# One attention layer with eight gates: where ScalarE's SiLU may begin, where two mixed heads are staged, and which transfer leaves first

## The chip, the cores and the metric

The kernel runs on one core of a Trainium2 chip. The metric is the device time of one execution in microseconds (us); lower is better. TensorE (PE) multiplies matrices, PEld is its weight load, VectorE (DVE) and ScalarE (ACT) do elementwise work, GpSimd (POOL) does a little of it and issues accumulating transfers, and SyncE (SP) issues most DMAs.

## What is computed

One layer (DEPTH is 1) of a trunk on 512 positions of width 2048, in float32. The reference, cut to its core:

```
h    = rms_norm(x, norm_g)
proj = h @ w_in                      # 2048 -> 8192: qA kA vA gA | qB kB vB gB
ya   = stick_breaking_attention(split_heads(qa, 8), split_heads(ka, 8), split_heads(va, 8))
yb   = chunk_band_attention(split_heads(qb, 8), split_heads(kb, 8), split_heads(vb, 8),
                            q_norm_g, k_norm_g, rel_bias)
mixed = concat([merge_heads(ya) * silu(ga), merge_heads(yb) * silu(gb)])
x     = x + mixed @ w_out            # 2048 -> 2048
```

Stick-breaking attention has no softmax: it takes log-sigmoids, a reversed running sum along the keys and one exponential. The chunked attention normalizes queries and keys per head, adds a bias by clipped distance and takes a softmax.

## The kernel before

The input projection is cut into 32 units of 256 columns, `u = 4 * g + kind`: eight groups g (two heads each), and in each group the kinds query, key, value and gate. The result of a unit is a tile `c` of 128 x 2 x 512. Products are Strassen-Winograd: seven half-size products in the place of eight, with sums of weight blocks (`s1` to `s4`) and of activation blocks (`T1` to `T4`) made on DVE. Every operand is split into a high part (a copy by ACT into the type `fp32r`) and a low part (the remainder, a subtraction by DVE), and a product is up to three matmuls. So a block of weights is ready for PE when ACT's cast (L571, for later steps L450) and behind it DVE's subtraction (L572, L454) are done.

**The running chain.** Units 3 to 30 of the sequence are "major": they go through seven stages p0 to p6, each a full product of 4 x 4 matmuls (L831 with 512 columns, L833 with 256). Stages accumulate in three banks of PSUM: p0, p2, p4 and p6 go on in one bank, p1 and p3 in a second, p5 in a third. Between them, `chain(m)` copies intermediate sums out, into a workspace `c` of four parts in the arena (`CMB`):

- `c0` (L593): after p0, and p2 may not start before it.
- `c3` (L596): after p1, and p3 may not start before it.
- `c2` (L599): after p2, and p4 may not start before it.
- The first and second of the three DVE joins (L601) after p3 and p4; p6 waits for the second one. Then the third after p5, the copy `c1` (L612) after p6, and the sum of the unit (L616).

The workspace `CMB` takes parts 20 to 28 of the arena (in units of 256 columns), and `UU`, which the units of the other kind use for their sums, parts 26 to 28: the last quarter of `CMB`. `chain` claims all of `CMB` at once before `c0`.

**Attention and gates** of a group run beside the units of the next group, in the gaps of the same engines: `prep_b` (norms of queries and keys, after a transpose), `v_turn` (transposed values, scaled by L1499), `score`, `turn`, `values`. `gates(g)` multiplies the gate tile by the norm of x on DVE (L1548) and then runs one ACT operation of three instructions (L1551, L1552): a load of the table that holds SiLU, the SiLU itself, and a load of the table with logarithm and exponential, which all other ACT work uses. `values` needs the gates for its last product; where they are not done yet, it first copies its bank to SBUF (L1532).

**The output projection** (units 32 to 35, `NU` being 32) multiplies the mixed heads, which went to DRAM (`mixd`) and come back as eight tiles j = 0 to 7. Each is loaded in two DMAs (L672, L673) into a staging place named by `HOME[j]`, and split there (L745, L746) into `x`. A place is free for its next user when the splits of its last one are done. The first output unit takes the heads in the order of j, eight products of three matmuls each.

**Order.** Nothing of the order is written out. A planner in the kernel (`schedule`) runs a clock with a cost for each operation; whenever an engine is free in that clock it takes the ready operation that is due first. `Op(engine, cost, fn, due)` is one such entry; without a due time it is due 4.5 us after it became ready (`LATE`), and `need(k, before)` is due so long before product k begins by the plan. What comes out is a fixed order on each engine, and each engine goes through its own in order.

**The start.** SP's first DMA loads the norm's gains `ng_t` (L130); then come, by due time, the first weights and the tiles of x. The two halves of x's first tile are issued on ACT's queue (L672, L673). Eight matmuls on zeros (L1562) run while they come in.

Of the kernel before, what the change touches and what calls it, by code (L numbers as in the profile page):

```python
# [11 lines left out]
AF = mybir.ActivationFunctionType  # L12
# [62 lines left out]
def trunk_kernel(ctx: ExitStack, tc: tile.TileContext, xT, xn, wi, wqk, wo, ng, qg, kg, rel, out):  # L75
# [50 lines left out]
    banks = ps.tile([P, 8, S], F32, tag="banks", name="banks")  # L126
    halves = banks.rearrange("p a (b c) -> p (a b) c", c=H)
    mixd = [dp.tile([P, S], F32, tag=f"mixd{i}", name=f"mixd{i}") for i in range(2 * NG)]

    sp.dma_start(ng_t, ng)  # L130

    KB = 256
    arena = single([P, 28 * KB], "arena")
# [8 lines left out]
    def avail(r):  # L142

        return all(r[1] <= x[0] or x[1] <= r[0] for x in taken.values())

    def claim(key, r):
        assert avail(r), (key, r, taken)
        taken[key] = r
        return arena[:, r[0]:r[1]] if r[0] < 100 * KB else parts[:, r[0] - 100 * KB:r[1] - 100 * KB]
# [39 lines left out]
    def AC(w, fn, due=None, n=1):  # L189
        return Op("ACT", (0.085 + 0.85e-3 * w) * n, fn, due)  # L190
# [389 lines left out]
    def chain(m):  # L580
        u = MAJOR[m]
        b = [banks[:, major_bank(u, p), :] for p in (0, 1, 5)]
        k = [at_step[stage(m, p)] for p in range(NP)]
        there = lambda p: lambda: ("stage", m, p) in done

        def free(p):
            x = major_bank(u, p)
            del holder[2 * x], holder[2 * x + 1]

        yield there(0)  # L590
        yield lambda: avail(CMB)
        c = claim(("cmb", m), CMB).rearrange("p (a b) -> p a b", a=4)
        yield AC(512, lambda: act.copy(c[:, 0, :], b[0]), need(k[2], AHEAD[5]))  # L593
        done.add(("before", m, 2))
        yield there(1)
        yield AC(512, lambda: act.copy(c[:, 3, :], b[1]), need(k[3], AHEAD[5]))  # L596
        done.add(("before", m, 3))
        yield there(2)
        yield AC(512, lambda: act.copy(c[:, 2, :], b[0]), need(k[4], AHEAD[5]))  # L599
        done.add(("before", m, 4))  # L600
        join = lambda i, x, y, op=ALU.subtract: lambda: dve.tensor_tensor(out=c[:, i, :], in0=x, in1=y, op=op)  # L601
        yield there(3)
        yield DV(512, join(2, b[1], c[:, 2, :]), clock[0] + 3)
        free(1)
        yield there(4)
        yield DV(512, join(3, c[:, 3, :], b[0]), need(k[6], AHEAD[6]))
        done.add(("before", m, 6))
        yield there(5)
        yield DV(512, join(0, b[2], c[:, 0, :], ALU.add), clock[0] + 3)
        free(5)  # L610
        yield there(6)
        yield AC(512, lambda: act.copy(c[:, 1, :], b[0]), clock[0] + 1)  # L612
        free(0)
        _, t = yield from result(u, 0)
        t_ = t.rearrange("p a (b c) -> p (a b) c", c=H)
        yield DV(1024, lambda: dve.tensor_tensor(out=t_, in0=c[:, :, :H], in1=c[:, :, H:], op=ALU.add), clock[0] + 1.5)  # L616
        unclaim(("cmb", m))
        done.add(("unit", u))

    X = {}  # L620
    XB, xb_tiles, staged = {}, {}, {}
    STAGE = "qk", "qk", "cq", "ck", "cv", "cg"

    HOME = "cq", "ck", "qk", "cq", "cv", "cg", "cq", "qk"
    SUMS = "qk", "qk", "qk", "qk", "qk", "ck", "qk", "ck"


# [12 lines left out]
    def activations(j, mixed):  # L640
# [23 lines left out]
        else:  # L664
# [5 lines left out]

        queue, engine = (act, "ACT") if j == 0 and not mixed else (sp, "SP")
        first = lambda: queue.dma_start(r.rearrange("p (a b) -> p a b", b=H)[:, 0:4:3, :], a.rearrange("p (a b) -> p a b", b=H))  # L672
        second = lambda: queue.dma_start(r[:, H:3 * H], b)  # L673
        one = ("B11",), f(h[:, :1]), f(l[:, :1])
        spawn(raw(j, mixed, Op(engine, 0.47, first, need(k, 10), lag=P * 2048), r, k,
                  [(0, 1) + one] + ([(3, 4, ("B12",)) + ((f(h[:, 6:]), f(l[:, 6:])) if not mixed else (None, None))] if not mixed or plain(NU, j) else []), j, not mixed, kt, dt), (0, 0, j))
        spawn(raw(j, mixed, Op(engine, 0.47, second, need(k + 2 * mixed, 9), lag=P * 2048), r, k + 2,
                  [(1, 3, ("B21", "B22"), f(h[:, 1:3]), f(l[:, 1:3]))], j + NJ, not mixed, kt, dt), (0, 0, j))
        yield lambda: all(("scaled", j, i, mixed) in done for i in (j, j + NJ))
        if mixed:  # L680
# [675 lines left out]
    def prep_b(g, kind, h):  # L1356

        n = head(g, h)
        yield lambda: "R" in done and ("unit", 4 * g + kind) in done
        yield lambda: all(("read", n - 1, k) in done for k in range(2)) if h else kind == 0 or ("read", n, 0) in done  # L1360
        yield lambda: not h or kind == 0 or ("read", n, 0) in done
        k, = yield from buffer("L")
        t_ = tmp([P, S], "L", "tm")
        i = yield from take(("forth", g, kind, h))
        f = C[g, kind][:, h, :]
        b = banks[:, i, :]

        def turn_(src):
            for t in range(NT):
                pe.transpose(b[:, t * P:(t + 1) * P], src[:, t * P:(t + 1) * P], ident)  # L1370

        yield M(0.5, lambda: turn_(f))

        def squares():
            for t in range(NT):
                act.activation(t_[:, t * P:(t + 1) * P], b[:, t * P:(t + 1) * P], AF.Square,
                               accum_out=ssq[:, kind, h, t:t + 1])

        yield Op("ACT", 2.0, squares)
        if kind == 0:  # L1380
            give(i)
        done.add(("read", n, kind))
        v, y = vq[:, kind, h, :], rq[:, kind, h, :]

        def norms():
            dve.tensor_tensor(out=v, in0=ssq[:, kind, h, :], in1=rstd2, op=ALU.mult)
            dve.tensor_scalar(out=v, in0=v, scalar1=1.0 / HD, scalar2=EPS, op0=ALU.mult, op1=ALU.add)

        yield DV(4, norms, n=3)
        yield from rsqrt(v, y, NT)  # L1390
        yield DV(4, lambda: dve.tensor_tensor(out=y, in0=y, in1=rstd, op=ALU.mult))
        if kind == 0:

            drop("L", k)

            def both():
                dve.tensor_scalar(out=yn[:, h, :], in0=y, scalar1=-1.0, scalar2=None, op0=ALU.mult)
                dve.reciprocal(out=yi[:, h, :], in_=y)

            yield DV(4, both, n=2)  # L1400
            done.add(("factor", n))
            return

        def scaled():
            for t in range(NT):
                act.activation(t_[:, t * P:(t + 1) * P], b[:, t * P:(t + 1) * P], AF.Copy, scale=y[:, t:t + 1])

        yield Op("ACT", 1.5, scaled)
        d = yield from qk_of(g, h)
        yield M(0.5, lambda: turn_(t_))  # L1410
        drop("L", k)
        yield from heads(n, 1, d, b, kg_t)
        give(i)
# [69 lines left out]
    def v_turn(g, h):  # L1483
        n = head(g, h)
        yield lambda: "R" in done and ("unit", 4 * g + 2) in done
        yield lambda: ("values", n - 1) in done if n else all(("staged", j, 0) in done for j in range(NJ))
        i = yield from take(("v", g, h))
        f = C[g, 2][:, h, :]
        b = banks[:, i, :]

        def fn():
            for t in range(NT):
                pe.transpose(b[:, t * P:(t + 1) * P], f[:, t * P:(t + 1) * P], ident)  # L1493

        yield M(0.5, fn)

        def scaled():
            for t in range(NT):
                act.activation(f[:, t * P:(t + 1) * P], b[:, t * P:(t + 1) * P], AF.Copy, scale=rstd[:, t:t + 1])  # L1499

        yield Op("ACT", 1.25, scaled)
        give(i)
        d = vv[n] = tmp([P, 2, S], "v", "v", F32R)
        yield AC(512, lambda: act.copy(d[:, 0, :], f))
        yield DV(512, lambda: dve.tensor_tensor(out=d[:, 1, :], in0=f, in1=d[:, 0, :].bitcast(F32), op=ALU.subtract))
        done.add(("v read", n))
        done.add(("v", g, h))

    def values(g, h):
# [32 lines left out]
        yield L_(P * 2048, lambda: sp.dma_start(mixd[(1 - g % 2) * NJ + g // 2 * 2 + h], f))  # L1542
        done.add(("store", g, h))

    def gates(g):
        yield lambda: "R" in done and ("unit", 4 * g + 3) in done
        f = C[g, 3]
        yield DV(1024, lambda: dve.tensor_tensor(out=f, in0=f, in1=R[:, None, :].to_broadcast([P, 2, S]), op=ALU.mult))  # L1548

        def silu():  # L1550
            act.activation(f, f, AF.Silu)  # L1551
            act.preload_act_table_set(TABLES)  # L1552

        yield Op("ACT", 3.7, silu)
        done.add(("gates", g))


# [10 lines left out]
                       pattern=[[-1, P]], channel_multiplier=1)  # L1568

    def constants():  # L1570
        yield Op("ACT", 1.28, lambda: act.preload_act_table_set(TABLES), -5.0)

        yield lambda: position[0] > 20

        def gains():
            sp.dma_start(qg_t, qg)
            sp.dma_start(kg_t, kg)

        yield Op("SP", 0.94, gains, 25.0)
        yield lambda: position[0] > 60  # L1580
        yield DV(1, lambda: dve.tensor_scalar(out=qgs, in0=qg_t, scalar1=SCALE, scalar2=None, op0=ALU.mult), 40.0)
# [71 lines left out]
```

## Time and profile before

| | us |
|---|---|
| median of 3 runs (913.51 to 915.98) | 914.37 |
| the profiled execution | 913.6 |
| its span, first to last instruction | 911.8 |
| PE busy | 899.8 (99%) |
| PEld busy | 802.1 (88%) |
| DVE busy | 768.9 (84%) |
| ACT busy | 636.7 (70%) |
| SiLU blocks on ACT: table load, SiLU, table load | 8, first at 102.3, last at 742.7 |

The span is the time between the first and the last instruction that the profiler saw; the execution takes 1.8 us more than that. A busy PE has matmuls in flight, which are pipelined: the start of one matmul to the start of the next says more than their lengths, and the idle time of PEld (the weight load ahead of each matmul) shows where PE waited for its operands.

### The profile page before, as it was taken

The numbers are of one execution on the slowest core, as the hardware profiler recorded it, in microseconds if no ns is written. First come the engines' busy times: TensorE is split into PE (matmuls) and PEld (weight loads), VectorE is DVE, ScalarE is ACT, GpSimd is POOL, SyncE is SP. The second block draws the span as 40 slices with busy tenths as digits, with TensorE's granted clock in tenths as the row PEclk, the third lists the DMA queues.
The fourth block names the chain that finished last, engine by engine and source line by source line (L and its number), as shares of the span: only waits on it lengthen the run. The fifth ranks groups of instructions, "written<-read, shape, count | busy, mean of one in ns | idle before, by whom it ended". The sixth has DMA issues, their size and how long they took to land.

```text
span 911.8 us, 15413 instructions
## 1 busy us (share of the span) xinstructions
PE 899.8 (99%) x5504; PEld 802.1 (88%) x5504; DVE 768.9 (84%) x1253; ACT 636.7 (70%) x1199; POOL 66.4 (7%) x91
## 2 busy tenths in 40 slices
PE   9999999999999999999999999999999999999997
PEld 6898888888888888888888888888888987899997
DVE  8989898788897887888978878889878988988785
ACT  8776967886687758775877587768868885534342
POOL 0001010000010100010001000010000000101011
PEclk9999999999999999999999999999999999999999
DMA  9677696566766886767667867676665536656371
GB/s 322 208 220 176 147 218 163 139 171 168 182 157 151 191 199 147 179 172 178 159 147 185 206 151 176 173 176 161 158 160 134 173 128 197 168 179 181 120 186 47
DMA packets 187549, 156.22 MB, mean 171 GB/s; under 512 B 9040, under 2 KB 157008, under 8 KB 187472
## 3 DMA queue, kind: packets, MB, share of 16 engines
q1 hardware_dynamic: 177264, 122.20, 44.0%
q0 software_dynamic: 9792, 32.51, 21.5%
q8 instruction: 43, 0.70, 0.3%
q10 hardware_dynamic: 416, 0.52, 0.2%
q14 instruction: 34, 0.28, 0.1%
HBM read 117.45 MB, written 8.39 MB: 138 GB/s over the span
## 4 chain that ended last, share of the span: by engine, by line
PE 85%; ACT 6%; DVE 5%; issue 2%; DMA 2%; DVEq 0%; SPq 0%; ACTq 0%
PE banks L831 35%; PE banks L760 18%; PE banks L833 17%; PE banks L758 9%; PE banks L821 2%; PE banks L1470 2%; DVE parts L572 1%; PE banks L1370 1%; ACT parts L571 1%; PE banks L822 1%; DMA arena<-in_wi 1%; ACT L1552 1%; DVE arena L540 1%; PE banks L1493 1%; ACT L1551 1%
## 5 line engine op out<-in xcount | busy, mean ns | idle before, releaser
L831 PE MATMUL banks<-x,parts 128*128 128x512 f32 x1568 | 502.5, 402 | 3.9 <-ACT arena L596 2.7
L833 PEld LDWEIGHTS banks<-x,parts 128*128 128x128 f32 x1568 | 294.5, 188 | 69.7
L833 PE MATMUL banks<-x,parts 128*128 128x256 f32 x1568 | 309.7, 279 | 0.0
L572 DVE TENSOR_TENSOR parts<-arena,parts 128x1024 fp32r<-128x1024 f32 x196 | 239.3, 1222 | 68.5 <-ACT parts L571 66.8
L571 ACT CAST parts<-arena 128x1024 fp32r<-128x1024 f32 x196 | 206.6, 1055 | 119.9 <-PE banks L831 85.1
L831 PEld LDWEIGHTS banks<-x,parts 128*128 128x128 f32 x1568 | 240.8, 189 | 6.4 <-ACT arena L596 4.0
L760 PE MATMUL banks<-parts,x 128*128 128x256 f32 (+1 forms) x672 | 135.1, 299 | 1.4 <-DVE x L746 1.4
L450 ACT CAST parts<-arena 128x1024 fp32r<-128x1024 f32 (+3 forms) x84 | 77.5, 928 | 75.9 <-PE banks L760 40.3
L760 PEld LDWEIGHTS banks<-parts,x 128*128 128x128 f32 x672 | 107.5, 191 | 5.9 <-DVE x L746 2.2
L454 DVE TENSOR_TENSOR parts<-arena,parts 128x1024 fp32r<-128x1024 f32 (+3 forms) x84 | 89.4, 1069 | 20.3 <-ACT parts L450 20.0
L758 PE MATMUL banks<-parts,x 128*128 128x256 f32 (+1 forms) x336 | 100.4, 299 | 0.0
L760 PE MATMUL banks<-x,parts 128*128 128x256 f32 (+1 forms) x320 | 75.6, 328 | 0.2 <-DVE parts L454 0.2
L540 DVE TENSOR_TENSOR arena<-arena 128x1024 f32<-128x1024 f32 x56 | 68.2, 1217 | 4.1 <-DMA arena<-in_wi 4.0
L758 PEld LDWEIGHTS banks<-parts,x 128*128 128x128 f32 x336 | 63.9, 190 | 3.2
L760 PEld LDWEIGHTS banks<-x,parts 128*128 128x128 f32 x320 | 53.9, 190 | 7.0 <-DVE parts L454 2.0
L532 POOL DMA_DIRECT2D arena<-arena x28 | 24.5, 875 | 415.9 <-DMA arena<-in_wi 119.9
L758 PE MATMUL banks<-x,parts 128*128 128x256 f32 (+1 forms) x160 | 52.8, 330 | 0.0
L601 DVE TENSOR_TENSOR arena<-banks,arena 128x512 f32<-128x512 f32 x56 | 38.3, 684 | 4.3 <-PE banks L833 4.1
L551 POOL DMA_DIRECT2D arena<-arena x28 | 24.4, 870 | 219.9 <-DVE parts L572 176.6
L616 DVE TENSOR_TENSOR c<-arena 128x1024 f32<-128x1024 f32 x28 | 34.1, 1217 | 0.3 <-ACT arena L612 0.2
L758 PEld LDWEIGHTS banks<-x,parts 128*128 128x128 f32 x160 | 30.5, 190 | 3.1 <-ACT parts L450 0.5
L1479 DVE TENSOR_TENSOR wtl<-banks,wth 128x128 fp32r<-128x128 f32 (+1 forms) x64 | 30.9, 483 | 1.6 <-ACT wth L1478 1.5
(210 smaller groups left out, 1156.1 us busy)
## 6 DMA issues: line engine op xcount, KB each, us to landing
arena<-in_wi SPq DMA_DIRECT2D x310, 256.0 KB, 4.2
arena<-arena POOLq DMA_DIRECT2D x56, 512.0 KB, 5.6
arena<-in_wo SPq DMA_DIRECT2D x64, 256.0 KB, 3.1
xs<-in_xn SPq DMA_DIRECT2D x16, 256.0 KB, 4.4
mixd<-c SPq DMA_DIRECT2D x16, 256.0 KB, 3.1
out<-co SPq DMA_DIRECT2D x16, 256.0 KB, 4.7
x<-mixd SPq DMA_DIRECT2D x12, 256.0 KB, 4.2
co<-in_xn POOLq DMA_DIRECT2D x12, 256.0 KB, 5.8
```

What stands on the lines that cost most here:

```text
L450: act.copy(whl[n, part][:, 0, c], t)
L454: yield DV(c.stop - c.start, lambda: dve.tensor_tensor(out=l[:, c], in0=t, in1=h[:, c].bitcast(F32), op=ALU.subtract), need(k, 0.5))
L540: add = lambda x, due: DV(1024, lambda: dve.tensor_tensor(out=r("A21"), in0=r("A21"), in1=r(x), op=ALU.add), due)
L571: yield AC(1024, lambda: act.copy(v[:, 0, :], t), need(k, AHEAD[3]))
L572: yield DV(1024, lambda: dve.tensor_tensor(out=v[:, 1, :], in0=t, in1=v[:, 0, :].bitcast(F32), op=ALU.subtract), need(k, AHEAD[4]))
L601: join = lambda i, x, y, op=ALU.subtract: lambda: dve.tensor_tensor(out=c[:, i, :], in0=x, in1=y, op=op)
L616: yield DV(1024, lambda: dve.tensor_tensor(out=t_, in0=c[:, :, :H], in1=c[:, :, H:], op=ALU.add), clock[0] + 1.5)
L758: pe.matmul(o, lh, rh, start=start, stop=False, **kw)
L760: pe.matmul(o, x, y, start=False, stop=stop and (x is ll) != early, **kw)
L831: pe.matmul(both, mats[n][:, 0, j, :], X[j][:, :, i, :], start=p in (0, 1, 5) and j == 0, stop=False, skip_group_check=True)
L833: pe.matmul(o[:, :H], mats[n][:, 1, j, :], X[j][:, 0, i, :], start=False, stop=j == NJ - 1, skip_group_check=True)
L1479: yield DV(w, lambda: dve.tensor_tensor(out=tl[:, blocks, :], in0=tv, in1=th[:, blocks, :].bitcast(F32), op=ALU.subtract))
```

## The change

Six edits:

1. `gates`: ahead of the SiLU block stands a condition `calm`. In a major unit it holds only in stages p3 to p5, once `c2` has been copied, the buffer for p5's weights is claimed and p5's weights are split. When it holds, the block is due at once.
2. `chain`: the workspace is claimed in quarters. `c0` waits for the first three, `c3` for the last one, which is the one that `UU` shares.
3. The four-part ACT operations of `prep_b` (squares, scaling) and `v_turn` (scaling) are four entries of the planner instead of one.
4. `HOME`: mixed heads 6 and 7 swap places; head 6 is staged in `qk`, head 7 in `cq`.
5. The start: `ng_t` is loaded from ACT's queue, behind the first half of x's first tile, whose second half goes to SP's queue.
6. Due times of the first loads of x: 9 instead of 10 for the first half of tile 1, 7.95 instead of 9 for the second half of tile 0.

```diff
-    sp.dma_start(ng_t, ng)
...
         yield there(0)
-        yield lambda: avail(CMB)
-        c = claim(("cmb", m), CMB).rearrange("p (a b) -> p a b", a=4)
+        def space(i):
+            w = (CMB[1] - CMB[0]) // 4
+            return CMB[0] + i * w, CMB[0] + (i + 1) * w
+
+        c = arena[:, CMB[0]:CMB[1]].rearrange("p (a b) -> p a b", a=4)
+        for i in (0, 1, 2):
+            yield lambda: avail(space(i))
+            claim(("cmb", m, i), space(i))
         yield AC(512, lambda: act.copy(c[:, 0, :], b[0]), need(k[2], AHEAD[5]))
         done.add(("before", m, 2))
         yield there(1)
+        yield lambda: avail(space(3))
+        claim(("cmb", m, 3), space(3))
         yield AC(512, lambda: act.copy(c[:, 3, :], b[1]), need(k[3], AHEAD[5]))
...
-    HOME = "cq", "ck", "qk", "cq", "cv", "cg", "cq", "qk"
+    HOME = "cq", "ck", "qk", "cq", "cv", "cg", "qk", "cq"
...
-        second = lambda: queue.dma_start(r[:, H:3 * H], b)
+        second = lambda: sp.dma_start(r[:, H:3 * H], b)
...
-        yield Op("ACT", 2.0, squares)
+        for t in range(NT):
+            yield Op("ACT", 0.5, lambda: act.activation(t_[:, t * P:(t + 1) * P], b[:, t * P:(t + 1) * P], AF.Square,
+                                                        accum_out=ssq[:, kind, h, t:t + 1]))
...
+    def calm():
+        u, r = steps_[program[min(position[0], len(program) - 1)][0]]
+        return not major(u) or 3 <= r < 6 and ("before", MAJOR.index(u), 4) in done and ("hl", NP * MAJOR.index(u) + 5) in done and ("w", step_of[u, 5]) in done
+
...
-        yield Op("ACT", 3.7, silu)
+        yield calm
+        yield Op("ACT", 3.7, silu, clock[0])
...
+        yield Op("ACT", 0.47, lambda: act.dma_start(ng_t, ng), -9.5)
         yield Op("ACT", 1.28, lambda: act.preload_act_table_set(TABLES), -5.0)
```

What it does to the order on the engines, at three places. First, ACT around the SiLU of the third group (`c_2786` before, `c_2802` now). `parts<-arena` is a cast of weights, L593, L596 and L599 are the chain's copies `c0`, `c3` and `c2`. Before:

```order
L571 CAST parts<-arena 128x1024
L593 COPY arena<-banks 128x512
L1478 CAST wth<-banks 128x128
L1337 ACTIVATE L<-banks,rstds 128x384
L1551 ACT_TABLE_LOAD
L1551 ACTIVATE c_2786<-c_2786 128x1024
L1552 ACT_TABLE_LOAD
L596 COPY arena<-banks 128x512
L571 CAST parts<-arena 128x1024
L1338 ACTIVATE L<-L 128x384
L599 COPY arena<-banks 128x512
```

In the changed kernel (the same copies are L597, L602 and L605 there, the casts L569):

```order
L597 COPY arena<-banks 128x512
L569 CAST parts<-arena 128x1024
L602 COPY arena<-banks 128x512
L1353 ACTIVATE W<-W 128x384
L569 CAST parts<-arena 128x1024
L605 COPY arena<-banks 128x512
L1499 ACTIVATE c_2563<-banks,rstd 128x128
L1553 ACT_TABLE_LOAD
L1553 ACTIVATE c_2802<-c_2802 128x1024
L1554 ACT_TABLE_LOAD
L569 CAST parts<-arena 128x1024
```

The block stood between `c0` and `c3` and now stands behind `c2`; the next instruction behind it is the cast of p6's weights. So it is at all seven blocks that fall into major units (the first one stood between `c3` and `c2` before, the other six between `c0` and `c3`); ahead of the block stand, behind `c2`, one to four short instructions of the attention. The eighth block, near 742 us, keeps its place but for one cast.

Second, ACT at the first chain, near 72 us. Before:

```order
L571 CAST parts<-arena 128x1024 x3
L1285 CAST qk_823<-c_500 128x512
L571 CAST parts<-arena 128x1024
L593 COPY arena<-banks 128x512
L596 COPY arena<-banks 128x512
```

In the changed kernel:

```order
L569 CAST parts<-arena 128x1024 x2
L597 COPY arena<-banks 128x512
L569 CAST parts<-arena 128x1024
L1292 CAST qk_823<-c_500 128x512
L569 CAST parts<-arena 128x1024
L602 COPY arena<-banks 128x512
```

The copy `c0` has moved ahead of the casts of p3's and p4's weights and of a cast of the attention; `c3` stays behind them.

Third, SP where the last mixed heads come back (`mixd14` is the first half of head 6, `mixd15` of head 7). Before:

```order
L673 DMA x51_7335<-mixd5_87 128x512
L672 DMA xm_7128<-mixd15_97 128x2x256
L673 DMA xm_7128<-mixd7_89 128x512
L381 DMA arena_99<-in_wo 128x512 x2
L672 DMA x61_7408<-mixd14_96 128x2x256
L673 DMA x61_7408<-mixd6_88 128x512
```

In the changed kernel:

```order
L680 DMA x51_7335<-mixd5_87 128x512
L679 DMA xm_7143<-mixd14_96 128x2x256
L680 DMA xm_7143<-mixd6_88 128x512
L379 DMA arena_98<-in_wo 128x512 x2
L679 DMA x71_7408<-mixd15_97 128x2x256
L680 DMA x71_7408<-mixd7_89 128x512
```

Head 7 was loaded ahead of head 6, though the products take head 6 first; now they come in the order in which they are taken. DVE's and ACT's splits of the two heads swap in the same way.

More of the change, by code (lines that the diff above doesn't have):

```diff
@@ L616, in chain @@
         yield DV(1024, lambda: dve.tensor_tensor(out=t_, in0=c[:, :, :H], in1=c[:, :, H:], op=ALU.add), clock[0] + 1.5)
-        unclaim(("cmb", m))
+        for i in range(4):
+            unclaim(("cmb", m, i))
         done.add(("unit", u))
@@ L672, in activations @@
         first = lambda: queue.dma_start(r.rearrange("p (a b) -> p a b", b=H)[:, 0:4:3, :], a.rearrange("p (a b) -> p a b", b=H))
-        second = lambda: queue.dma_start(r[:, H:3 * H], b)
+        second = lambda: sp.dma_start(r[:, H:3 * H], b)
         one = ("B11",), f(h[:, :1]), f(l[:, :1])
-        spawn(raw(j, mixed, Op(engine, 0.47, first, need(k, 10), lag=P * 2048), r, k,
+        spawn(raw(j, mixed, Op(engine, 0.47, first, need(k, 10 if mixed or j != 1 else 9), lag=P * 2048), r, k,
                   [(0, 1) + one] + ([(3, 4, ("B12",)) + ((f(h[:, 6:]), f(l[:, 6:])) if not mixed else (None, None))] if not mixed or plain(NU, j) else []), j, not mixed, kt, dt), (0, 0, j))
-        spawn(raw(j, mixed, Op(engine, 0.47, second, need(k + 2 * mixed, 9), lag=P * 2048), r, k + 2,
+        spawn(raw(j, mixed, Op("SP", 0.47, second, need(k + 2 * mixed, 7.95 if engine == "ACT" else 9), lag=P * 2048), r, k + 2,
                   [(1, 3, ("B21", "B22"), f(h[:, 1:3]), f(l[:, 1:3]))], j + NJ, not mixed, kt, dt), (0, 0, j))
@@ L1372, in prep_b @@
         yield M(0.5, lambda: turn_(f))
[L1374 to L1377, printed above, removed]
-        yield Op("ACT", 2.0, squares)
+        for t in range(NT):
+            yield Op("ACT", 0.5, lambda: act.activation(t_[:, t * P:(t + 1) * P], b[:, t * P:(t + 1) * P], AF.Square,
+                                                        accum_out=ssq[:, kind, h, t:t + 1]))
         if kind == 0:
@@ L1402, in prep_b @@
             return
[L1404 to L1408, printed above, removed]
+        for t in range(NT):
+            yield Op("ACT", 0.37, lambda: act.activation(t_[:, t * P:(t + 1) * P], b[:, t * P:(t + 1) * P], AF.Copy, scale=y[:, t:t + 1]))
         d = yield from qk_of(g, h)
@@ L1495, in v_turn @@
         yield M(0.5, fn)
[L1497 to L1501, printed above, removed]
+        for t in range(NT):
+            yield Op("ACT", 0.31, lambda: act.activation(f[:, t * P:(t + 1) * P], b[:, t * P:(t + 1) * P], AF.Copy, scale=rstd[:, t:t + 1]))
         give(i)
```

## The prediction

> **What bounds it now.** I read the page first, then what PEld waited for, then the timeline at each of those waits.
>
> ```profile
> PE 899.8 (99%) x5504; PEld 802.1 (88%) x5504; DVE 768.9 (84%) x1253; ACT 636.7 (70%) x1199; POOL 66.4 (7%) x91
> ```
>
> PE is in flight for 99% of the span and its instructions are the same in number after the change. So only time in which PE's stream stands still can be won. The table of waits lists it for the weight load, in us, times, longest:
>
> ```profile
> PEld banks L831 <- ACT arena L596: 4.0, 6, 0.8
> PEld banks L760 <- DVE x L746: 2.2, 2, 1.4
> PEld banks L760 <- DVE parts L454: 2.0, 5, 0.6
> ...
> PEld banks L831 <- ACT arena L593: 1.4, 1, 1.4
> ...
> PEld banks L758 <- DVE W L1344: 0.3, 1, 0.3
> PEld banks L821 <- ACT co L934: 0.2, 1, 0.2
> ```
>
> Four groups carry it: six waits for the chain's copy `c3` (L596), one for its first `c0` (L593), two for a mixed head (L746), five at the start (L454).
>
> **The six waits for c3.** The timeline at one of them:
>
> ```profile
> 284.97 1.28 ACT L1551 ACT_TABLE_LOAD   x1
> 286.26 1.06 ACT L1551 ACTIVATE c<-c 128x1024 f32<-128x1024 f32 x1
> 287.34 1.28 ACT L1552 ACT_TABLE_LOAD   x1
> ...
> 287.93 0.63 PE L831 MATMUL banks<-x,parts 128*128 128x512 f32 x2
> ...
> 288.64 0.59 ACT L596 COPY arena<-banks 128x512 f32<-128x512 f32 x1
> 289.12 1.05 ACT L571 CAST parts<-arena 128x1024 fp32r<-128x1024 f32 x1
> ...
> 289.27 0.73 PE L831 MATMUL banks<-x,parts 128*128 128x512 f32 x2 [0.48 <-ACT arena L596]
> ...
> 290.08 0.63 PE L831 MATMUL banks<-x,parts 128*128 128x512 f32 x2
> 290.20 1.23 DVE L572 TENSOR_TENSOR parts<-arena,parts 128x1024 fp32r<-128x1024 f32 x1 [4.75 <-ACT parts L571]
> ...
> 696.27 0.63 PE L831 MATMUL banks<-x,parts 128*128 128x512 f32 x2
> ...
> 696.97 0.63 PE L831 MATMUL banks<-x,parts 128*128 128x512 f32 x2
> ```
>
> The SiLU block holds ACT from 284.97 to 288.64, 3.67 us; `c3` stands behind it and p3 waits. A product takes 0.70 undisturbed (696.97 - 696.27), so a stage of four takes 2.8, less than the block. Here the product that waits loses 289.27 - 287.93 - 0.70 = 0.64 and the one after it 0.81 - 0.70 = 0.11, together 0.75. If the other five lose as this one does beside their share of the 4.0, the six lose 4.0 + 6 x 0.07 = 4.4.
>
> After the change the block starts behind `c2`. What is then due first on ACT is the cast of p6's weights, with DVE's low part behind it. From the end of p2, p6 begins three stages later: 3 x 2.8 = 8.4. On the way stand `c2` with its hand-over (0.1 + 0.59), at five of the seven blocks one or two short instructions (up to 0.9, one like the 0.59 copy and 0.3), the block 3.67, the cast 1.05 and the low part 1.23 with two hand-overs (0.2): 7.7. That leaves 0.7 in hand, and PE's own attention work, which lies between stages, only adds to it. At the first and the last block three and four short instructions stand there, some 1.6, which leaves nothing in hand; a tenth or two at those is in what I give back below. DVE's side: the second join runs after p4, so not before 5.6, and where it stands ahead of the low part the sum is 5.6 + 0.1 + 0.7 + 1.23 = 7.6, no tighter. So I take 4.4 gained. Bounds: one more DVE instruction of 1.23 ahead of the low part would overrun by 0.5, at seven blocks 3.5 given back; at the other end nothing is.
>
> The same rows price a rule of the Trainium skill that speaks against the change. "ScalarE: Activation LUTs", What ACT_TABLE_LOAD costs, counts about 2.66 us for every switch to a different set, a load of 1283 ns and a drain of 1380 ns. The load agrees with the 1.28 here; no drain lies between these rows, since ACT's next instruction begins 0.02 behind a load. By that rule this part would lose 8.9 where I take 4.4 gained, which is the last rival below.
>
> **The first chain.** Its rows:
>
> ```profile
> 74.73 2.00 ACT L571 CAST parts<-arena 128x1024 fp32r<-128x1024 f32 x2 [3.09 <-DVE arena L540]
> ...
> 75.89 1.21 DVE L572 TENSOR_TENSOR parts<-arena,parts 128x1024 fp32r<-128x1024 f32 x1
> ...
> 76.98 0.60 PE L1493 MATMUL banks<-ident,c 128*128 128x128 f32 x4
> 77.02 0.41 DVE L1005 TENSOR_TENSOR c<-banks,arena 128x256 f32<-128x256 f32 x1
> ...
> 77.16 1.04 ACT L571 CAST parts<-arena 128x1024 fp32r<-128x1024 f32 x1
> ...
> 78.10 0.57 ACT L593 COPY arena<-banks 128x512 f32<-128x512 f32 x1
> ...
> 78.73 0.73 PE L831 MATMUL banks<-x,parts 128*128 128x512 f32 x2 [1.15 <-ACT arena L593]
> ```
>
> p2 could have begun behind the transposes, near 77.4, and begins at 78.73. `c0` waited for the whole workspace, whose last quarter the old unit still read until 77.43 (77.02 + 0.41), and then for a cast. Now it needs only the first three quarters and stands behind the first of the two casts of 74.73, so it can run near 75.8 and be done at 76.4; p2's low part ends at 77.10. The gain is the 1.4 of the table. `c3` still waits for the old unit, then for two casts and a cast of q: 75.8 + 0.6 + 1.0 + 0.6 + 1.0 + 0.6 = 79.6, against p3's new begin at 77.4 + 2.8 = 80.2. If that fails, up to 1.4 comes back.
>
> **Mixed heads 6 and 7.**
>
> ```profile
> 761.35 0.53 SPq L672 DMA_DIRECT2D xm<-mixd  x1
> ...
> 762.08 0.39 PE L758 MATMUL banks<-parts,x 128*128 128x512 f32 x1
> ...
> 766.16 0.39 PE L758 MATMUL banks<-parts,xbwth 128*128 128x512 f32 x1
> ...
> 769.14 0.53 SPq L672 DMA_DIRECT2D x<-mixd  x1
> ...
> 772.96 0.39 PE L758 MATMUL banks<-parts,x 128*128 128x512 f32 x1
> ...
> 774.72 1.22 DVE L454 TENSOR_TENSOR parts<-arena,parts 128x1024 fp32r<-128x1024 f32 x1
> ...
> 775.85 0.68 DVE L746 TENSOR_TENSOR x<-x,x 128x512 fp32r<-128x512 f32 x1
> ...
> 779.01 0.39 PE L758 MATMUL banks<-parts,xbwtl 128*128 128x512 f32 x1
> ```
>
> Six products on one head take 766.16 - 762.08 = 4.08; on head 6 they take 779.01 - 772.96 = 6.05. The loss is 1.97, against 2.2 in the table; I take 1.9. Head 6 was loaded at 769.14, head 7 at 761.35. After the swap head 6 has the early place, 11.6 before PE asks for it. Head 7 gets head 6's times: its weights are ready at 775.94, its last low part at 776.53. PE asks for head 7 eight products behind 772.96, at 772.96 + 8 x 0.68 = 778.4, so 1.9 are left. Gain 1.9; were the slack gone, up to 1.9 would come back.
>
> **The start.**
>
> ```profile
> 0.75 0.39 SPq L130 DMA_DIRECT2D ng_t<-in_ng  x1
> ...
> 1.20 0.42 SPq L381 DMA_DIRECT2D arena<-in_wi  x1
> ...
> 1.24 0.49 ACTq L673 DMA_DIRECT2D xq<-in_xT  x1
> ...
> 3.87 0.51 ACT L751 ACTIVATE x<-xq,ng_t 128x256 fp32r<-128x256 f32 x1 [0.82 <-DMA xq<-in_xT]
> ...
> 4.29 0.41 ACT L450 CAST parts<-arena 128x256 fp32r<-128x256 f32 x1
> ...
> ng_t<-in_ng SPq DMA_DIRECT2D x1, 8.0 KB, 2.4
> ```
>
> The first weights leave at 0.75 instead of 1.20, but the first product hung on x: the scale ran at 3.87 when x came, and the cast of the weights right behind it at 4.29. `ng_t` now leaves at about 1.24 and lands 2.4 later, at 3.64, 0.23 ahead of its use. The second weights are 0.45 earlier too, which takes a little from the five waits (2.0). I take 0.2 gained. Bounds: 2.0 gained if all five go; 0.5 lost if the move of `ng_t` (0.49) comes through whole. The Trainium skill ("DMA: Bandwidth & Descriptors", Queues, rings and completion order) says that each DMA engine goes round between the queue rows it has work for; an earlier load of weights would then slow x's first tile, which no row here separates.
>
> **Edits at nothing.** The split four-part operations issue the same instructions; `values` copies its bank three times more (0.59 each) and DVE reads those from SBUF; ACT, at 70%, hides both. The stores behind the gates move by a few positions of SP's queue.
>
> **The sum.** 4.4 + 1.4 + 1.9 + 0.2 = 7.9. The new order will have small waits of its own: the last two rows of the table, 0.5 together, are of that kind, and I give that back. 7.4 from the profiled execution's 913.6 is 906.2; its time lies 0.8 under the median 914.37, so the median should come to 907.0.
>
> **The rivals.** (a) p6's weights are late by up to 0.5 at the seven blocks, because DVE is 84% busy and takes something else first: 3.5 comes back, 910.5. Against it: the 0.7 in hand. (b) Head 7 waits in head 6's place: DVE has hardly a gap there, but its rows leave 1.9; 908.9. (c) The planner only moves the waits: what ACT puts off by the block is owed to some copy later, and all but a microsecond or two comes back, 912 to 915. For it: each block is still 3.67 of ACT. Against: between blocks ACT idles 30%. (d) Slower, by one mechanism: the backlog behind the block reaches p6 2.3 late at each of seven blocks, 1.6 beyond the slack, 11.2 in all: 907.0 + 11.2 = 918.2. It decides against the change from 1.8 late (7 x 1.1 = 7.7), and wants ACT to be behind already when the block starts, which the condition on p5's weights speaks against. (e) A switch of tables drains ACT for about as long as it loads; two more times 1.3 would put p6 1.9 beyond its slack: 907.0 + 7 x 1.9 = 920. The rows show 3.67 for the whole block, so I give it next to nothing. That is the rule of the Trainium skill above.
>
> **How the numbers follow.** All three places won as worked out: 0.58, 905.0 to 909.0 with the bounds of the start. (a) 0.16, (b) 0.12, (c) 0.09, (d) and (e) 0.05, nearly all of it (d). The first three are faster by over 0.3% (2.7 us, about what can be told from no change): 0.86. (c) is the same, 0.09. The range takes the first three in: 905.0 to 911.5.
>
> **What would show it.** In the changed kernel's waits, PEld's rows for `c3` and for L746's head 6 are gone, and none stands for the casts' low parts behind a block (L570). Around each block ACT runs `c2`, block, cast, and p6 starts without idle time. The first chain's p2 starts right behind the transposes. Six products on head 6 take 4.1, and head 7 as well. The first product starts within 0.3 of 5.05. A row "PEld banks L831 or so <- DVE parts L570" of several us, seven times, would be (a) or (d); a wait for head 7 would be (b); a wait for `ng_t` ahead of the first scale would cost the start.

## The result, and the profile after

The changed kernel takes 909.35 us (median of 6 runs, 907.76 to 909.99) against 914.1 for the kernel before (6 runs, 913.51 to 915.98). The ratio is 0.9942 with a 95% interval of 0.9928 to 0.9955, so 4.8 us are won. Forecast were 907.0, in a range of 905.0 to 911.5. The direction and the range hold; of the 7.1 that the median should have lost, a third did not come. The profiled execution took 909.28 with a span of 907.5.

PE's line on the page and the table of what PEld waited for (us, times, longest), both of the changed kernel. L765 and L767 are now the matmuls of the start (L758 and L760 before), L838 and L840 those of the major units (L831 and L833), L448 and L569 casts, L452 and L570 low parts:

```profile
PE 898.7 (99%) x5504; PEld 802.2 (88%) x5504; DVE 769.2 (85%) x1253; ACT 639.7 (70%) x1202; POOL 66.2 (7%) x91
```

```profile
PEld banks L765 <- ACT parts L448: 1.6, 1, 1.6
...
PEld banks L840 <- DVE parts L570: 1.1, 2, 0.6
PEld banks L838 <- issue: 1.0, 2, 0.5
PEld banks L1471 <- ACT W L1456: 0.7, 2, 0.5
PEld banks L767 <- DVE parts L452: 0.7, 1, 0.7
```

The six waits for `c3`, the one for `c0` and the two for a mixed head are all gone from it. In their place stand a wait of 1.6 ahead of the first product and a handful of half-microsecond waits that were not there before.

**A block of SiLU after the change.** The timeline of ACT, and then of DVE, around the third group's block, the one whose timeline the prediction shows:

```profile
290.69 0.58 ACT L605 COPY arena<-banks 128x512 f32<-128x512 f32 x1
291.17 0.37 ACT L1499 ACTIVATE c<-banks,rstd 128x128 f32<-128x128 f32 x1
291.54 1.28 ACT L1553 ACT_TABLE_LOAD   x1
292.84 1.06 ACT L1553 ACTIVATE c<-c 128x1024 f32<-128x1024 f32 x1
293.92 1.28 ACT L1554 ACT_TABLE_LOAD   x1
295.21 1.05 ACT L569 CAST parts<-arena 128x1024 fp32r<-128x1024 f32 x1
```

```profile
296.30 1.23 DVE L570 TENSOR_TENSOR parts<-arena,parts 128x1024 fp32r<-128x1024 f32 x1 [0.54 <-ACT parts L569]
```

It reads as the prediction had it: `c2` (L605), one short instruction, the block from 291.54 to 295.21, which is again 3.67, the cast of p6's weights, and its low part done at 297.53. PE began p3 at 290.78, so p6 follows three stages of 2.8 later, near 299.2; 1.7 are in hand. PE's stream runs on without a wait.

**The first chain.** ACT's, DVE's and PE's timelines near 78 us (all times stand 1.3 later here than before, which the start has cost):

```profile
77.53 0.58 ACT L597 COPY arena<-banks 128x512 f32<-128x512 f32 x1
```

```profile
77.72 1.21 DVE L570 TENSOR_TENSOR parts<-arena,parts 128x1024 fp32r<-128x1024 f32 x1
```

```profile
78.28 0.63 PE L838 MATMUL banks<-x,parts 128*128 128x512 f32 x2
78.98 0.50 PE L840 MATMUL banks<-x,parts 128*128 128x256 f32 x2
```

`c0` is done at 78.11 and p2 starts at 78.28, behind p1. Then it stands for 0.24 more (two matmuls of such a product take 0.46, so the third was due at 78.74 and began at 78.98), because the low part of its weights ends at 78.93. DVE has become what p2 waits for. Where 1.31 was lost before, 0.24 is now.

**The start.** The timeline of the first ten microseconds, and the table of DMA issues in them (its last number is the time from issue to landing):

```profile
0.75 0.39 SPq L379 DMA_DIRECT2D arena<-in_wi  x1
...
1.24 0.49 ACTq L1574 DMA_DIRECT2D ng_t<-in_ng  x1
...
5.29 0.51 ACT L758 ACTIVATE x<-xq,ng_t 128x256 fp32r<-128x256 f32 x1 [2.24 <-DMA ng_t<-in_ng]
5.70 0.39 ACT L448 CAST parts<-arena 128x256 fp32r<-128x256 f32 x1
...
6.14 0.80 PE L765 MATMUL banks<-x,parts 128*128 128x512 f32 x1 [0.90 <-ACT parts L448]
7.10 1.22 PE L767 MATMUL banks<-x,parts 128*128 128x512 f32 x2 [0.16 <-DVE parts L452]
8.12 0.63 PE L765 MATMUL banks<-x,parts 128*128 128x512 f32 x1
8.55 1.05 PE L767 MATMUL banks<-x,parts 128*128 128x512 f32 x2
```

```profile
ng_t<-in_ng ACTq DMA_DIRECT2D x1, 8.0 KB, 4.0
```

The gains landed 4.0 after their issue, at 5.24, and not 2.4 after it, at 3.64. ACT's first scale waited for them and no longer for x; the first product began at 6.14 where it began at 5.05 before. And then comes something that the prediction had no term for: PE is slow. From 8.12 to 8.55 is one matmul, 0.43, and from 8.55 the next two take 0.85 (the next stands at 9.40), though nothing is waited for. Such a matmul takes 0.23 in the steady stream. The zeros ahead of the first product stand 0.43 apart too, so PE was slow from its first matmul on. Full pace is there only at 9.7, against 6.6 before.

### The profile page after: what moved, and what is told of

It reads as the page before. It is cut to its first block, busy times and chain, and to the rows that moved or that the text cites. A ratio compares the mean times of both kernels' runs of the same rounds, so it can differ in the third digit from the quotient of the medians.

```text
span 907.5 us, 15449 instructions
## 1 busy us (share of the span) xinstructions
PE 898.7 (99%) x5504; PEld 802.2 (88%) x5504; DVE 769.2 (85%) x1253; ACT 639.7 (70%) x1202; POOL 66.2 (7%) x91
## 4 chain that ended last, share of the span: by engine, by line
PE 89%; DVE 4%; ACT 3%; DMA 2%; issue 1%; SPq 0%; DVEq 0%; ACTq 0%
PE banks L838 36%; PE banks L767 20%; PE banks L840 18%; PE banks L765 10%; DMA arena<-in_wi 2%; PE banks L1471 2%; PE banks L828 2%; DVE parts L570 1%; PE banks L1377 1%; ACT parts L569 1%; PE banks L1494 1%; PE banks L829 1%; DVE arena L538 1%; DMA ng_t<-in_ng 0%; DVE arena L607 0%
## 5 line engine op out<-in xcount | busy, mean ns | idle before, releaser
L838 PE MATMUL banks<-x,parts 128*128 128x512 f32 x1568 | 501.4, 401 | 0.7 <-DVE arena L607 0.7
L840 PEld LDWEIGHTS banks<-x,parts 128*128 128x128 f32 x1568 | 294.3, 188 | 70.5 <-DVE parts L570 1.1
L840 PE MATMUL banks<-x,parts 128*128 128x256 f32 x1568 | 309.9, 279 | 0.3 <-DVE parts L570 0.2
L570 DVE TENSOR_TENSOR parts<-arena,parts 128x1024 fp32r<-128x1024 f32 x196 | 239.0, 1220 | 64.8 <-ACT parts L569 64.4
L569 ACT CAST parts<-arena 128x1024 fp32r<-128x1024 f32 x196 | 206.1, 1053 | 115.2 <-PE banks L838 89.0
L838 PEld LDWEIGHTS banks<-x,parts 128*128 128x128 f32 x1568 | 240.7, 189 | 2.0 <-issue 1.0
L767 PE MATMUL banks<-parts,x 128*128 128x256 f32 (+1 forms) x672 | 134.5, 298 | 0.0
L448 ACT CAST parts<-arena 128x1024 fp32r<-128x1024 f32 (+3 forms) x84 | 77.2, 928 | 68.4 <-PE banks L767 37.2
L767 PEld LDWEIGHTS banks<-parts,x 128*128 128x128 f32 x672 | 107.6, 191 | 3.7
L452 DVE TENSOR_TENSOR parts<-arena,parts 128x1024 fp32r<-128x1024 f32 (+3 forms) x84 | 89.1, 1067 | 13.8 <-ACT parts L448 13.2
L765 PE MATMUL banks<-parts,x 128*128 128x256 f32 (+1 forms) x336 | 100.4, 299 | 0.0
L538 DVE TENSOR_TENSOR arena<-arena 128x1024 f32<-128x1024 f32 x56 | 68.3, 1219 | 8.9 <-DMA arena<-in_wi 8.5
L767 PE MATMUL banks<-x,parts 128*128 128x256 f32 (+1 forms) x320 | 75.7, 329 | 0.2 <-DVE parts L452 0.2
L765 PEld LDWEIGHTS banks<-parts,x 128*128 128x128 f32 x336 | 64.0, 190 | 3.2
L767 PEld LDWEIGHTS banks<-x,parts 128*128 128x128 f32 x320 | 54.4, 192 | 5.8 <-DVE parts L452 0.7
L765 PE MATMUL banks<-x,parts 128*128 128x256 f32 (+1 forms) x160 | 53.4, 334 | 0.9 <-ACT parts L448 0.9
L607 DVE TENSOR_TENSOR arena<-banks,arena 128x512 f32<-128x512 f32 x56 | 38.2, 683 | 8.0 <-PE banks L840 4.3
L765 PEld LDWEIGHTS banks<-x,parts 128*128 128x128 f32 x160 | 30.8, 192 | 4.5 <-ACT parts L448 1.6
```

Of the source, the lines that this page charges most:

```text
L448: act.copy(whl[n, part][:, 0, c], t)
L452: yield DV(c.stop - c.start, lambda: dve.tensor_tensor(out=l[:, c], in0=t, in1=h[:, c].bitcast(F32), op=ALU.subtract), need(k, 0.5))
L538: add = lambda x, due: DV(1024, lambda: dve.tensor_tensor(out=r("A21"), in0=r("A21"), in1=r(x), op=ALU.add), due)
L569: yield AC(1024, lambda: act.copy(v[:, 0, :], t), need(k, AHEAD[3]))
L570: yield DV(1024, lambda: dve.tensor_tensor(out=v[:, 1, :], in0=t, in1=v[:, 0, :].bitcast(F32), op=ALU.subtract), need(k, AHEAD[4]))
L765: pe.matmul(o, lh, rh, start=start, stop=False, **kw)
```

## Where the time went

Start-to-start times of matmuls beyond the steady pace, added up by place, give in the two profiled executions (913.6 and 909.28, 4.3 apart):

| | lost before | lost after | won | forecast |
|---|---|---|---|---|
| start (when the 301st matmul, the 293rd behind the zeros, begins: 62.86, 64.16) | | | -1.3 | 0.2 |
| first chain | 1.31 | 0.24 | 1.1 | 1.4 |
| waits for `c3` | 4.2 | 0 | 4.2 | 4.4 |
| mixed heads | 1.9 | 0 | 1.9 | 1.9 |
| small waits of the order | 0.3 | 2.05 | -1.75 | -0.5 |

The column "won" comes to 4.15. Its first row is the least certain: in eight profiled executions with the start of before, that matmul begins anywhere from 62.55 to 63.86. The five small waits of after are at 90.7 (0.53), 113.7 (0.35), 229.8 (0.47), 231.8 (0.26) and 698.1 (0.44). Rows of three of them, from the timelines:

```profile
89.38 1.23 DVE L538 TENSOR_TENSOR arena<-arena 128x1024 f32<-128x1024 f32 x1 [1.31 <-DMA arena<-in_wi]
...
91.35 0.70 PE L838 MATMUL banks<-x,parts 128*128 128x512 f32 x2 [0.37 <-DVE arena L607]
```

```profile
114.29 0.51 PE L840 MATMUL banks<-x,parts 128*128 128x256 f32 x2 [0.18 <-DVE parts L570]
```

```profile
230.43 0.70 PE L838 MATMUL banks<-x,parts 128*128 128x512 f32 x2 [0.31 <-DVE arena L607]
```

At 91.35 PE waits for a join (L607). The join stands on DVE behind a sum of weights (L538) that itself waited 1.31 for a load of weights: DVE goes in its order, so a late load holds up a join that has nothing to do with it. At 230 the same pair stands 3 us apart, and that the load is the cause there is only argued. At 114.29 it is the low part of p6 behind the first block, the place with three short instructions ahead of the block, which the prediction gave no slack.

## The experiments

Each was timed beside the kernel before, whose median was 913.52 beside the first four, 913.69 beside the next four, 913.66 beside the next three and 913.6 beside the last. A ratio is against before, with its 95% interval in brackets.

### The start put back

The changed kernel with the start of before: gains on SP first, both halves of x's first tile on ACT, the old due times.

```diff
+    sp.dma_start(ng_t, ng)
-        second = lambda: sp.dma_start(r[:, H:3 * H], b)
+        second = lambda: queue.dma_start(r[:, H:3 * H], b)
-        yield Op("ACT", 0.47, lambda: act.dma_start(ng_t, ng), -9.5)
```

> The changed kernel with the start of before (gains first on SP, both halves of x's first tile on ACT's queue, old due times). Theory Q (the gains, queued behind 256 KB of x on ACT's queue, land late, and all waits for them): the first product starts at 5.05 again instead of 6.14, and with the waits behind it the time falls by 1.5, to about 907.8. Rival L (the later stall of the start comes from late second weights, and the later parts absorb a start that is earlier): the first product moves, the time stays at 909.3.

Measured 907.94 (906.97 to 908.75), ratio 0.9932 [0.9917, 0.9947]. From its timeline:

```profile
3.99 0.51 ACT L760 ACTIVATE x<-xq,ng_t 128x256 fp32r<-128x256 f32 x1 [0.96 <-DMA xq<-in_xT]
...
4.85 0.49 PE L767 MATMUL banks<-x,parts 128*128 128x512 f32 x1
```

The gains landed 2.1 after their issue, the scale waited for x again, and the first product stood at 4.85. So the new start takes back a part of what the kernel gained elsewhere; the two medians are 1.4 apart, and the intervals of the two ratios still overlap. In the profiled execution little of it shows: the 293rd product begins at 63.86, only 0.3 before the changed kernel's, since PE then waits for weights, 0.57 of it near 18.2. The new start alone, below, is the firmer measure.

### Only the gains back on SP

The changed kernel with `sp.dma_start(ng_t, ng)` ahead of all else and no load of gains on ACT; x's second half stays on SP.

> The changed kernel with only the gains' load put back to the head of SP's queue; the second half of x's first tile stays on SP. Theory Q: the gains land near 3.2, the scale then waits for x alone (it landed 3.6 after 0.75 in the changed kernel), so it starts near 4.35 and the first product near 5.2; the time falls by about 1.0, to 908.3. Rival C (the transfers of the start crowd one another, and whichever is needed last is late): x lands where the gains did, near 5, and the time stays at 909.3.

Measured 908.93 (908.33 to 909.41), ratio 0.9943 [0.9931, 0.9956]: no different from the changed kernel. The first product stood at 5.03, but the second weights came later on SP, and two waits of 0.57, at 7.9 and 17.9, took the place of what was won.

### The gains ahead of x on ACT's queue

The changed kernel with the gains' due time at -10.5 instead of -9.5, so that they leave ACT's queue before x.

> The changed kernel with the gains ahead of x's first half on ACT's queue instead of behind it. Theory Q: the gains land about 2.4 after 0.75, x leaves at 1.24 and lands near 4.9; the first product starts near 5.7 and the time is 908.9. Rival S (ACT's queue is slow for 64-byte rows, wherever they stand in it): the gains still take 4 us, land near 4.8, x behind them later still, and the time is 909.5 or more.

Measured 909.43 (907.97 to 910.04), ratio 0.9946 [0.9932, 0.996]. From its table of DMA issues:

```profile
xq<-in_xT ACTq DMA_DIRECT2D x1, 256.0 KB, 4.1
ng_t<-in_ng ACTq DMA_DIRECT2D x1, 8.0 KB, 2.8
```

The same 8 KB from the same queue land in 2.8 instead of 4.0 when nothing stands before them. So the place behind 256 KB of x makes the gains late, and not the queue nor the form of the load. The transfers themselves show it too: in the changed kernel the rows of x start on this queue between 2.38 and 3.86, and the 128 rows of the gains between 3.85 and 4.61. Nothing is won, since x now leaves at 1.19 and lands 4.1 later, and the first product waits for it until 5.94. A wait of 1.4 near 90 us in this one execution shows how the place of the 0.53 above varies.

### The start alone

The kernel before with the new start (edits 5 and 6) and nothing else.

> The kernel before with the new start alone. Theory Q: first product at 6.1, time 1.5 over before, about 915.6. Rival L: under 914.7.

Measured 915.58 (913.76 to 917.93, 11 runs), ratio 1.0017 [1.0006, 1.0027]: slower by 1.6 by the ratio (0.5 to 2.5). The old waits stand as before, and two new rows are the start's:

```profile
PEld banks L829 <- ACT arena L594: 4.0, 6, 0.8
...
PEld banks L756 <- ACT parts L448: 1.6, 1, 1.6
```

The gains took 4.0, the first product stood at 6.15, and matmuls 0.427 apart went on until 10.3.

### The condition on the SiLU alone

The kernel before with `calm` and the due time of the block (edit 1).

```diff
+        yield calm
-        yield Op("ACT", 3.7, silu)
+        yield Op("ACT", 3.7, silu, clock[0])
```

> The kernel before with the condition ahead of the SiLU block alone (edit 1). Theory W (the six waits for c3 were worth what the weight load's rows say, and new small waits cost about 2): PEld's row for c3 is gone, 4.4 won, 1 to 2 given back behind the blocks; the time is 2.5 to 3.5 under before. Rival M (the waits only move): PEld waits for casts or low parts near the seven blocks, 3 us or more in all, and the time is within 1 of before.

Measured 909.39 (908.64 to 910.41), ratio 0.9949 [0.9937, 0.9961]: 4.7 won by the ratio (3.6 to 5.8), 4.3 by the medians. Its waits keep the mixed head and `c0`, and the row for `c3` is gone:

```profile
PEld banks L760 <- DVE x L746: 1.9, 2, 1.2
PEld banks L831 <- ACT arena L593: 1.6, 1, 1.6
```

This one edit gains nearly as much as the whole change, with the forecast 4.4 inside its interval. It brought more than I expected of it alone.

### The quarters of the workspace alone

The kernel before with edit 2.

> The kernel before with the workspace claimed in quarters alone (edit 2). Theory W: the wait of 1.4 for c0 near 77 becomes a wait of 0.3 for p2's low part; the time is 1.1 under before. Rival N (what is won at 77 is lost again within a unit, since the old unit's reading is only overtaken): no gain.

Measured 914.36 (913.72 to 915.27, 11 runs), ratio 1.0005 [0.9997, 1.0014]. At the first chain 0.22 is lost, now to a low part. The waits for `c3` fall from six to four, but two for `c2` come in place of the others:

```profile
PEld banks L840 <- ACT arena L604: 2.2, 4, 0.7
PEld banks L840 <- ACT arena L607: 2.0, 2, 1.2
```

L604 is `c3` here, L607 is `c2`. At 106 us the block of SiLU and a cast run ahead of `c2`, and p4 waits 1.2 for it; near 225 and 252 PE waits 0.7 and 1.0 for attention that has come late. The edit lets the planner lay out everything behind it anew, and what it gains at 77 us it gives away there.

### The mixed heads alone

The kernel before with heads 6 and 7 swapped in `HOME` (edit 4).

> The kernel before with heads 6 and 7 swapped in HOME alone (edit 4). Theory W: six products on head 6 take 4.1 instead of 6.05, head 7 waits for nothing; 1.9 under before. Rival N: head 7 waits, or DVE's later splits do, and less than 1 is left.

Measured 911.6 (910.39 to 913.37, 12 runs), ratio 0.9976 [0.9968, 0.9985]: 2.2 won (1.4 to 2.9), for a forecast of 1.9. Both waits for L746 are gone, and none for head 7 came, so rival (b) is refuted. The waits for `c3` stand as they were:

```profile
PEld banks L831 <- ACT arena L596: 4.0, 6, 0.8
```

### The split four-part operations alone

The kernel before with edit 3.

> The kernel before with the four-part ACT operations as four entries alone (edit 3). Theory W: the chain's copies can pass between the four parts, but in before none of the waits over 0.15 stood behind such an operation; the six c3 waits stay, time within 1 of before. Rival F (the split is what frees the chain's copies): several c3 waits shrink, 2 or more are won.

Measured 913.83 (912.63 to 915.24, 11 runs), ratio 0.9999 [0.9991, 1.0008]. I had costed the edit at nothing, and nothing it is, but not since it does nothing. In the profiled execution the group for `c3` is gone, and these stand in its place:

```profile
PEld banks L833 <- DVE parts L572: 2.1, 1, 2.1
PEld banks L831 <- ACT arena L593: 1.9, 1, 1.9
...
PEld banks L758 <- ACT xbwth L745: 1.3, 1, 1.3
PEld banks L760 <- DVE xbwth L746: 1.0, 1, 1.0
```

With ACT's order laid out anew, the copies `c3` are in time, but a low part is late, the first `c0` (L593) is later than before (1.9, where it was 1.4), and a mixed head is late at another place. That is rival (c), waits only moved, for this edit.

### The condition and the heads together

Edits 1 and 4 on the kernel before, with its start.

> The kernel before with the SiLU's condition and the swap of heads 6 and 7, the two edits that won alone (4.3 and 2.1 by medians); start, quarters and four-part operations as before. Theory A (the edits add): 6.4 to 6.9 under before, near 907.0, and under the changed kernel. Rival I (they get in each other's way, since the planner lays the rest anew): 908.5 or more.

Measured 906.83 (906.69 to 908.07), ratio 0.9928 [0.9915, 0.994]. The two gains add: 4.3 and 2.1 by the medians alone, 6.8 together. The largest waits that are left:

```profile
PEld banks L760 <- DVE parts L454: 1.9, 4, 0.7
PEld banks L831 <- ACT arena L593: 1.6, 1, 1.6
```

Two of the six edits beat the whole change: by 2.5 us by the bare medians, 2.1 with each median held against the kernel before beside it, 1.3 by the ratios, whose intervals overlap.

### And the quarters

The same with edit 2.

> The same with the workspace claimed in quarters too. Theory A: the wait of 1.5 near 77 goes, 906.0. Rival R (each new layout brings waits of its own, as the quarters alone did): within 1 of the run without quarters, with new waits of 1 in all at places that no edit names.

Measured 906.81 (906.67 to 907.36), ratio 0.9924 [0.9912, 0.9936], no different from the last one. The wait of 1.6 for `c0` is gone, and three of 0.3 to 0.4 came, at 89, 112 and 136 us, two of them as this row:

```profile
PEld banks L840 <- issue: 0.8, 2, 0.4
```

Those at 89 and 112 are the ones that the changed kernel has at 90.7 and 113.7, and the version without the quarters lacks them, so they come with the quarters. The other three of the changed kernel's five (229.8, 231.8 and 698.1) are absent here and present, with 0.45, 0.27 and 0.42, in the changed kernel with the start of before. That version differs from this one by edit 3 alone, so these three come with the split operations.

### More zeros ahead of the first product

The changed kernel with eleven matmuls on zeros instead of eight, so that PE has no idle time before its late first product.

```diff
-WARM = 8
+WARM = 11
```

> The changed kernel with 11 matmuls on zeros instead of 8, so that PE is busy until 6.2, when the first product can start. Theory G (PE's pace halves after the idle 1.1 us ahead of the first product, 427 ns a matmul instead of 230 until 9.6): the matmuls from 7.5 on start 230 ns apart, and the time falls by about 0.8, to 908.5. Rival P (the slow pace lasts until a fixed time or for a fixed number of products): 427 ns until 9 or later, time 909.3.

Measured 907.2 (906.92 to 908.88), ratio 0.9927 [0.9914, 0.9941]. From PE's timeline:

```profile
6.33 0.63 PE L765 MATMUL banks<-x,parts 128*128 128x512 f32 x1
7.10 0.81 PE L767 MATMUL banks<-x,parts 128*128 128x512 f32 x2
7.74 0.39 PE L765 MATMUL banks<-x,parts 128*128 128x512 f32 x1
```

The first product comes later than in the changed kernel (6.33), the second waits as it did (7.10), and yet full pace is there from 7.5 on instead of 9.7. The kernel is 1.4 (by the ratios, whose intervals overlap) to 2.1 (by the medians) faster for three matmuls that compute nothing. The transfers are those of the changed kernel, so the slow pace lasts so long there because of the gap in PE's work ahead of the first product, not because of what the transfers bring.

### Fewer zeros in the kernel before

The kernel before with `WARM = 5`: the same idle time, with every transfer as it was.

> The kernel before with five matmuls on zeros ahead of the first product instead of eight (they stand 0.427 us apart, so PE is idle from about 3.6 to the first product at 5.0, some 1.3 us, as it is in the changed kernel with its first product at 6.1). Nothing else differs, the DMAs least of all. Theory G (idle time of PE ahead of the first product leaves PE at half pace for some 3.5 us, whatever the transfers do): matmul starts 427 ns apart until 8.5 to 9.5 instead of about 6.3, and the time 0.8 to 1.5 above the kernel before, near 914.6. Rival P (PE at half pace in the changed kernel because its operands come late and singly, the zeros make no difference): the starts are 230 ns apart from about 6.3 as before, and the time stays within 0.5 of the kernel before.

Measured 914.14 (913.23 to 915.92, 11 runs), ratio 1.001 [1.0, 1.0019]. PE's timeline, and a row of the waits:

```profile
4.95 0.80 PE L758 MATMUL banks<-x,parts 128*128 128x512 f32 x1 [0.98 <-ACT parts L450]
...
9.23 0.63 PE L758 MATMUL banks<-x,parts 128*128 128x512 f32 x1
9.66 1.05 PE L760 MATMUL banks<-x,parts 128*128 128x512 f32 x2
```

```profile
PEld banks L760 <- DVE parts L454: 0.4, 1, 0.4
```

The pace is as theory G has it, and slow for longer than it said: 9.23 to 9.66 is one matmul, and they stay 0.43 apart until 10.94. The rival, that the operands make it slow, is refuted, since the transfers are those of before. The cost is less than I expected, 0.5 by the medians (0.9 by the ratio) instead of 0.8 to 1.5, and its interval reaches down to nothing. The waits for low parts at the start, 2.0 before, fall to 0.4, so what PE loses in pace it would partly have stood waiting for anyway; that this makes up the difference is argued, not shown.

## Why the prediction was right, and where not

- **The waits for `c3`, 4.4.** Right, alone (4.3 to 4.7) and in place. The block is still 3.67 long, the cast of p6 follows it, and the slack held at six of seven blocks. At the seventh, the first one, the version with edits 1 and 4 has no such wait, so it hangs on the order that the quarters bring. Rivals (a) and (d) needed p6 late at seven blocks; it is 0.35 late at one. For rival (e) the trace shows 0.01 to 0.02 between SiLU and a load, or a load and the next instruction. The Trainium skill's drain of 1380 ns at each switch ("ScalarE: Activation LUTs", What ACT_TABLE_LOAD costs) is in none of these rows, and the 8.9 that it would have cost did not come.
- **The mixed heads, 1.9.** Right: 2.2 alone, no wait for head 7.
- **The first chain, 1.4.** Right in kind, 0.3 too large. I had DVE's low part end before PE asked for it; it ends 0.2 after. With the 1.3 of the start taken off, PE asks at 76.97 and not near 77.4, since the transposes no longer stand ahead of p2, and the low part ends at 77.62 and not at 77.10: DVE's sum of weights, from which ACT casts, comes later itself (75.33, against 73.49 before). I had left DVE's order as it was.
- **The start, 0.2 won with bounds of 2.0 won and 0.5 lost.** This term failed, outside its bounds: 1.3 lost in the profile, 1.6 with the start alone. The first product, which was to start within 0.3 of 5.05, came at 6.14. Two steps of it were wrong. The landing time of `ng_t` was taken from a row in which it stood first in its queue, 2.4, and used for a place behind 256 KB of x, where it takes 4.0. And the bound priced a late first product by its own delay, and had no term for the slow pace behind the gap. That pace seems the larger part: where the first product was late (5.94, 6.33) but the pace full by 5.26 and 7.29, the 293rd product begins at 62.91 and 63.58, inside the 62.55 to 63.86 of the start of before; where the pace was full only from 9.6 on, it begins at 64.04 to 64.62 (two and three executions, so the share is an estimate). The sentence that a wait for `ng_t` ahead of the first scale would cost the start names what then happened, but no bound held it.
- **Edits at nothing.** The split operations cost nothing, alone. That they, and the quarters, lay out the order anew was in the working only as the 0.5 given back.
- **What the new order gives back, 0.5.** Too small: 2.05 stand in the profile, against 0.3 of this kind that went. I took the two smallest rows of before as the measure of a new order's waits. The versions with edits 1 and 4, with the quarters added, and with the split added to that show where the five come from: two with the quarters, three with the split.
- **The range and the chances.** The range reached up to 911.5 for the sake of rivals (a) and (b), neither of which came. It held 909.35 all the same, by two mis-sized terms that a bound should have carried. For the case that all three places won, the prediction said 905.0 to 909.0, and 909.35 lies above that. So the three large terms were right by their mechanism, and that the range held the time is in part luck.

## What to carry to other kernels

A landing time is read from a row in which the load has the same place in its queue: a small load behind a large one lands after the large one, not in its own time. Where a kernel warms PE up, what warms it must last until the first product is ready, so a start that delays this product needs its warming longer by as much. And where a planner lays out the order, an edit is to be tried alone before it is kept: here two edits of six made all of the gain, the two of the start together cost 1.6 alone, and the other two won nothing alone and brought small waits of their own.

## What the runs showed of the hardware

**A slow pace that the table of stretches doesn't show.** In the changed kernel's table by stretches (first the stretch and its length, then the busy time and number of each engine, then PE's clock, the DMA share and GB/s), the stretch that holds the slow matmuls has a granted clock of 1.00:

```profile
5.00:11.00 6.00, 4.94 (x14) 3.43 (x14) 5.52 (x14) 5.51 (x14) 0.00 (x0) 1.00 0.95 323
```

Matmuls stood 0.427 apart until 9.4, and 0.23 from 9.7 on, nearly a factor of two. The trace's own record of the granted clock begins only at 9.59, with full clock; nothing stands ahead of it, and the table shows such time as 1.00. In the three kernels with 0.9 to 1.2 us without matmuls, after 2.3 to 3.6 us of them, that record begins at 9.59 (the changed one), 10.60 (the start alone) and 10.97 (fewer zeros). In the ten executions whose zeros ran up to the first product or nearly, it begins between 4.35 and 7.59. The exception is the kernel with the gains first on ACT's queue: idle for 0.9, and yet its record begins at 5.26, and its matmuls show no step of 0.43 behind the first product.

The Trainium skill ("TensorE: Matmul & The Clock Gate", Part 1) describes a clock gate that gives half the clock until PE has been busy for a window of about 3.4 us, and a window that runs freely, whatever the kernel does. The factor agrees, and so does the record: its stretches of full clock last 897.705, 901.119 or 904.532 us in all 14 traces, steps of 3.41. Counted back in such steps (an estimate, for the record holds no earlier window), a whole one of the exception, 1.85 to 5.26, is filled by the zeros, which run from 1.47 to 5.25; in the changed kernel the one from 2.77 to 6.18 holds the gap, and the one from 6.18 to 9.59 is the first without it. A window need not be full to the last: with the split operations alone it runs from 0.94 to 4.35, and the zeros began at 1.47. So by this reading the same start can come out fast or slow from one execution to the next.

**A small load behind a large one.** The same 8 KB took 1.8 to 2.4 at the head of SP's queue, 2.8 at the head of ACT's and 4.0 behind 256 KB on ACT's, in all three executions with that place.
